# Row-wise logsumexp on one core: one Ln of ScalarE moved from before the last exp to after it, with the load sizes and shares redrawn

## The chip, the core and the metric

The kernel runs on one core of a Trainium2 chip. The metric is the device time of one execution in microseconds (us); of a kernel, the median of its runs. Three parts of the core do the work here: the 16 DMA engines bring the input from HBM into SBUF (the on-chip memory of 128 partitions), ScalarE (ACT in the profile) takes exponentials and logarithms, and VectorE (DVE) adds up rows. SyncE (SP) issues the transfers. TensorE has no part in it, and GpSimd (POOL) only sets a few constants at the start.

## What is computed

The input is `x`, 32 x 512 rows of 1024 fp32 numbers, and the output is one number for each row:

```python
x_max = np.max(x, axis=axis, keepdims=True)
return x_max.squeeze(axis) + np.log(np.sum(np.exp(x - x_max), axis=axis))
```

The kernel computes `log(sum(exp(x)))` without taking the maximum off; for the numbers drawn (standard normal) this is the same value. There are 16384 rows, 67.1 MB, and each partition holds 128 rows that lie one after the other in HBM. So a "row" below means one row in each of the 128 partitions: 4 KB per partition, 0.5 MB in all.

## The kernel before

The 128 rows are cut into 17 loads ("chunks") by the list `CHUNKS` (lines 11 to 16). An entry `(r, n_dve, parts, by_halves)` says: the chunk has `r` rows; VectorE sums the first `n_dve` of them, after ScalarE has exponentiated them in `parts` pieces; ScalarE sums the other `r - n_dve` itself, one row at a time. Early chunks have up to 16 rows, the last four have one row each.

*The ring.* The chunks land in `ring`, 51 rows of SBUF (line 54). The loop on lines 76 to 81 places them one behind the other and begins again at row 0 when a chunk doesn't fit. `load(i)` (lines 92 to 102) is issued on SyncE's queue. It first waits until whatever sat in its rows has been summed: for `dve_done` (VectorE's count of finished sums) or `act_done` (ScalarE's count of finished instructions), as the list `busy` noted. All loads share this one queue and are issued in order. Each has a semaphore of its own, `landed[i]`.

*The work on a chunk* (lines 126 to 172) is issued in program order on each engine; there is no scheduler, the order is written out by hand. ScalarE waits for `landed[i]` (line 135) and runs `exp` in place on the rows of each piece (line 137). VectorE waits for that piece and sums it, with one `reduce_sum` over all its rows (line 157), or, if `by_halves` is set, with one instruction per row (line 144) that adds the two halves of the row and accumulates the result; in the profile the latter is a CUSTOM_DVE_ANT_0 with a short DVE_READ_ACCUMULATOR2_ANT behind it. For the rows that ScalarE keeps, `exp` has an accumulator output (line 164): an ACTIVATE of 1024 elements and an ACTIVATION_READ_ACCUMULATOR that writes the row's sum. These sums go to `sums` in SBUF, except for the last `LATE` = 4 rows, whose sums go to `late` in PSUM (lines 111 to 115), a second on-chip memory.

*The logarithms.* `take_logs` (lines 104 to 109) puts on ScalarE's queue a wait for `act_done`, a wait for `dve_done` and a `Ln` of a stretch of sums, written to `res`. There are three:

- ahead of chunk `LN_AT` = 7, for the rows of chunks 0 to 5 (81 rows; lines 130 to 132);
- ahead of the last chunk, for all rows since then but the last four (43 rows; lines 133 and 134). Its `act_done` wait is for what was done before the first of the last four chunks, its `dve_done` wait for all of VectorE's sums;
- after the last chunk, for the last four rows (line 174). It waits for the last sum.

Then SyncE waits for the full count of `act_done` and stores `res`, 64 KB, with one transfer (lines 175 and 176). The activation tables for Exp and Ln are loaded once (line 122), and the load of chunk 0 is moved ahead of the start barrier (lines 184 to 192).

Of the kernel before, what the change touches and what calls it, by code (L numbers as in the profile page):

```python
# [8 lines left out]


CHUNKS = [
    (4, 4, 1, False), (15, 15, 1, False), (16, 16, 2, False), (16, 16, 2, False),
    (16, 15, 2, False), (14, 14, 2, False), (13, 12, 2, False), (9, 8, 1, False),
    (7, 7, 1, True), (5, 4, 1, True), (4, 3, 1, True), (3, 3, 1, False), (2, 2, 1, True),
    (1, 0, 1, False), (1, 0, 1, False), (1, 0, 1, False), (1, 0, 1, False),
]
RING_ROWS = 51

LN_AT = 7
LN_LAG = 1  # L20


LATE = 4


@with_exitstack
def kernel(
    ctx: ExitStack,
    tc: tile.TileContext,
    x: bass.AP,  # L30
    axis: bass.AP,
    out: bass.AP,
):
    nc = tc.nc
    P = nc.NUM_PARTITIONS

    assert axis in (-1, len(x.shape) - 1), f"only last-axis reduction supported, got {axis}"

    x_flat = x.flatten_outer_dims()
    N, D = x_flat.shape  # L40
    assert N % P == 0
    NB = N // P
    assert sum(r for r, *_ in CHUNKS) == NB

    fp32 = mybir.dt.float32
    Exp = mybir.ActivationFunctionType.Exp
    Ln = mybir.ActivationFunctionType.Ln
    Add = mybir.AluOpType.add
    AX = mybir.AxisListType.X

    x_v = x_flat.rearrange("(p t) d -> p t d", p=P)
    out_v = bass.AP(tensor=out.tensor, offset=out.offset, ap=[[NB, P], [1, NB]])

    ring = nc.alloc_sbuf_tensor("ring", [P, RING_ROWS, D], fp32).ap()
    sums = nc.alloc_sbuf_tensor("sums", [P, NB], fp32).ap()
    late = nc.alloc_psum_tensor("late", [P, 512], fp32).ap()
    res = nc.alloc_sbuf_tensor("res", [P, NB], fp32).ap()

    landed = [nc.alloc_semaphore(f"landed{i}") for i in range(len(CHUNKS))]
    act_done = nc.alloc_semaphore("act_done")  # L60
    dve_done = nc.alloc_semaphore("dve_done")
    stored = nc.alloc_semaphore("stored")
    used = sorted(sem.num for sem in [*landed, act_done, dve_done])
    assert used == list(range(used[0], used[0] + len(used)))

    tc.close()
    tc.compile()  # L70
    symbolic, nc._always_lower_symbolic_ap = nc._always_lower_symbolic_ap, False


    place = []
    row = slot = 0
    for r, *_ in CHUNKS:
        if slot + r > RING_ROWS:
            slot = 0
        place.append((slot, row))
        slot += r  # L80
        row += r

    busy = [(0, 0)] * RING_ROWS
    acts = dves = 0

    def cuts(n, parts):
        ends = [-(-n * k // parts) for k in range(parts + 1)]
        return [(lo, hi) for lo, hi in zip(ends, ends[1:]) if lo < hi]  # L90

    def load(i):
        (s, row), r = place[i], CHUNKS[i][0]
        act_wait = max(a for a, _ in busy[s : s + r])
        dve_wait = max(d for _, d in busy[s : s + r])
        if dve_wait:
            nc.sync.wait_ge(dve_done, dve_wait)
        if act_wait:
            nc.sync.wait_ge(act_done, act_wait)
        nc.sync.dma_start(out=ring[:, s : s + r], in_=x_v[:, row : row + r]).then_inc(  # L100
            landed[i], 16
        )

    def take_logs(lo, hi, src, dve_wait, act_wait):
        nonlocal acts
        nc.scalar.wait_ge(act_done, act_wait)
        nc.scalar.wait_ge(dve_done, dve_wait)
        nc.scalar.activation(out=res[:, lo:hi], in_=src, func=Ln).then_inc(act_done, 1)  # L108
        acts += 1

    late_row = place[-LATE][1]
    assert not any(n_dve for _, n_dve, _, _ in CHUNKS[-LATE:])

    def total(t):
        return late[:, t - late_row : t - late_row + 1] if t >= late_row else sums[:, t : t + 1]

    body = nc.main_func.blocks[-1]
    n_barrier = len(body.instructions)
    load(0)
    n_early = len(body.instructions)  # L120

    nc.scalar.preload_act_table_set("natural_log_exp_and_others")  # L122

    logged = 0
    done_before = [(0, 0)]
    for i, (r, n_dve, parts, by_halves) in enumerate(CHUNKS):
        if i:
            load(i)
        s, row = place[i]
        if i == LN_AT:  # L130
            logged = place[i - LN_LAG][1]
            take_logs(0, logged, sums[:, :logged], *done_before[i - LN_LAG])
        if i == len(CHUNKS) - 1:
            take_logs(logged, late_row, sums[:, logged:late_row], *done_before[-LATE])
        nc.scalar.wait_ge(landed[i], 16)
        for lo, hi in cuts(n_dve, parts):
            nc.scalar.activation(  # L137
                out=ring[:, s + lo : s + hi], in_=ring[:, s + lo : s + hi], func=Exp
            ).then_inc(act_done, 1)
            acts += 1  # L140
            nc.vector.wait_ge(act_done, acts)
            if by_halves:
                for j in range(lo, hi):
                    nc.vector.tensor_tensor_reduce(  # L144
                        out=ring[:, s + j, : D // 2],
                        in0=ring[:, s + j, : D // 2],
                        in1=ring[:, s + j, D // 2 :],
                        scale=1.0,
                        scalar=0.0,
                        op0=Add,  # L150
                        op1=Add,
                        accum_out=sums[:, row + j : row + j + 1],
                    ).then_inc(dve_done, 1)
                    dves += 1
                    busy[s + j] = (0, dves)
            else:
                nc.vector.reduce_sum(  # L157
                    out=sums[:, row + lo : row + hi], in_=ring[:, s + lo : s + hi], axis=AX
                ).then_inc(dve_done, 1)
                dves += 1  # L160
                for j in range(lo, hi):
                    busy[s + j] = (0, dves)
        for j in range(n_dve, r):
            nc.scalar.activation(  # L164
                out=ring[:, s + j],
                in_=ring[:, s + j],
                func=Exp,
                accum_out=total(row + j),
            ).then_inc(act_done, 1)
            acts += 1  # L170
            busy[s + j] = (acts, 0)
        done_before.append((dves, acts))

    take_logs(late_row, NB, late[:, : NB - late_row], dves, acts)
    nc.sync.wait_ge(act_done, acts)
    nc.sync.dma_start(out=out_v, in_=res).then_inc(stored, 16)


    nc.sync.sem_clear(range(used[0], used[-1] + 1))
    nc.sync.wait_ge(stored, 16)  # L180
    nc.sync.sem_inc(stored, -16)


    first = nc.main_func.blocks[0]
    head, work = first.instructions, body.instructions
    for ins in work[n_barrier:n_early]:
        at = next(
            k for k, i in enumerate(head) if i.engine == ins.engine and i.opcode == "Drain"
        )
        head.insert(at, ins)  # L190
    first.instructions = head
    body.instructions = work[:n_barrier] + work[n_early:]

    nc._always_lower_symbolic_ap = symbolic
# [33 lines left out]
```

The softmax here doesn't subtract the row's maximum and nothing guards it: scores larger than these inputs give would overflow.

## Time and profile before

| what | value |
|---|---|
| median of 9 runs | 162.32 us (162.24 to 162.68) |
| the profiled execution's own time | 162.32 us |
| its span, first to last instruction | 161.0 us |
| VectorE busy | 121.0 us, 46 instructions |
| ScalarE busy | 115.1 us, 40 instructions |
| packets of the load and store queue, share of 16 DMA engines' span | 97.2% |
| input read, mean rate over the span | 67.11 MB, 417 GB/s |
| chain that ended last | DMA 48%, DVE 29%, ACT 20% |

How to read it: the span is what the profile sees, and 1.3 us of the execution's own time lie around it. An engine's busy time is the time in which it had at least one instruction running. The chain of waits is followed back from the last instruction, at each step to what released it; its shares say which engine was the late one at that step, and a transfer that had been issued long before still counts from its issue. In the timeline each line is a start and a duration in us, and the text in brackets says how long the engine had been idle before it and what ended the idle time. Instructions on one engine overlap a little at their ends, so the distance from one start to the next is somewhat shorter than a duration.

### The profile page before, as it was taken

How to read it: one execution, taken by the hardware profiler on the slowest of the kernel's cores; microseconds unless marked ns; L12 is line 12 of the kernel's file. 1: busy time of each engine (PE TensorE's matmuls, PEld its weight loads, DVE VectorE, ACT ScalarE, POOL GpSimd, SP SyncE). 2: the span in 40 equal slices, each digit the busy share in tenths (PEclk: the TensorE clock that was granted, in tenths of full speed). 3: DMA queues.
4: the chain of work that ended last, by engine and by line, in shares of the span. 5: the costliest groups of instructions: out<-in, count | busy, mean ns of one | idle time of the engine just before them, and what ended most of it. 6: DMA issues, size and time to landing. Idle time of an engine off the chain costs nothing.

```text
span 161.0 us, 149 instructions
## 1 busy us (share of the span) xinstructions
DVE 121.0 (75%) x46; ACT 115.1 (71%) x40; POOL 0.2 (0%) x4
## 2 busy tenths in 40 slices
DVE  0028000003999999999999699999999999999892
ACT  3170006995089960999429993999199999999995
POOL 0000000000000000000000000000000000000000
DMA  7999889979979979979979999999999999999990
GB/s 273 493 488 473 366 382 521 456 326 521 456 326 521 440 342 521 440 342 521 440 309 456 456 456 440 423 423 423 422 421 421 433 442 401 436 415 428 407 402 29
DMA packets 2592, 67.18 MB, mean 417 GB/s; under 512 B 288, under 2 KB 416, under 8 KB 928
## 3 DMA queue, kind: packets, MB, share of 16 engines
q1 hardware_dynamic: 2592, 67.18, 97.2%
HBM read 67.11 MB, written 0.07 MB: 417 GB/s over the span
## 4 chain that ended last, share of the span: by engine, by line
DMA 48%; DVE 29%; ACT 20%; issue 0%
DMA ring<-in_x_dram 48%; DVE sums L157 29%; ACT ring L137 17%; ACT ring L164 3%; ACT res L108 0%
## 5 line engine op out<-in xcount | busy, mean ns | idle before, releaser
L157 DVE TENSOR_REDUCE sums<-ring 128x8 f32<-128x8192 f32 (+5 forms) x14 | 111.2, 7994 | 36.9 <-ACT ring L137 36.8
L137 ACT ACTIVATE ring<-ring 128x8192 f32<-128x8192 f32 (+6 forms) x18 | 104.4, 5835 | 42.9 <-DMA ring<-in_x_dram 42.8
L144 DVE CUSTOM_DVE_ANT_0 ring<-ring 128x512 f32<-128x512 f32 x16 | 9.9, 684 | 0.0
L164 ACT ACTIVATE ring<-ring 128x1024 f32<-128x1024 f32 x9 | 9.3, 1041 | 0.0
L122 ACT ACT_TABLE_LOAD x1 | 1.3, 1283 | 1.4 <-PEq L70 1.4
L164 ACT ACTIVATION_READ_ACCUMULATOR ring<-ring 128x1 f32 x9 | 1.6, 173 | 0.0
L144 DVE DVE_READ_ACCUMULATOR2_ANT sums<- 128x1 f32 x16 | 1.3, 80 | 0.0
L108 ACT ACTIVATE res<-sums 128x81 f32<-128x81 f32 (+1 forms) x2 | 0.5, 247 | 0.0
L108 ACT ACTIVATE res<-late 128x4 f32<-128x4 f32 x1 | 0.2, 174 | 0.0
L209 POOL MEMSET const-bfloat16-1.0<- 128x1 bf16 x1 | 0.1, 102 | 0.0
L209 POOL MEMSET const-uint8-127<- 128x1 uint8 x1 | 0.1, 102 | 0.0
L209 POOL MEMSET const-float32-0.0<- 128x1 f32 x1 | 0.1, 99 | 0.2 <-issue 0.2
L209 POOL MEMSET const-float32-1.0<- 128x1 f32 x1 | 0.1, 99 | 0.0
## 6 DMA issues: line engine op xcount, KB each, us to landing
ring<-in_x_dram SPq DMA_DIRECT2D x1, 7680.0 KB, 24.2
ring<-in_x_dram SPq DMA_DIRECT2D x1, 7168.0 KB, 28.6
ring<-in_x_dram SPq DMA_DIRECT2D x1, 6656.0 KB, 35.7
ring<-in_x_dram SPq DMA_DIRECT2D x1, 4608.0 KB, 20.3
ring<-in_x_dram SPq DMA_DIRECT2D x2, 2048.0 KB, 16.1
ring<-in_x_dram SPq DMA_DIRECT2D x1, 3584.0 KB, 28.3
ring<-in_x_dram SPq DMA_DIRECT2D x1, 2560.0 KB, 27.3
ring<-in_x_dram SPq DMA_DIRECT2D x4, 512.0 KB, 27.1
```

Source lines behind the costliest of these rows:

```text
L108: nc.scalar.activation(out=res[:, lo:hi], in_=src, func=Ln).then_inc(act_done, 1)
L122: nc.scalar.preload_act_table_set("natural_log_exp_and_others")
L137: nc.scalar.activation(out=ring[:, s + lo : s + hi], in_=ring[:, s + lo : s + hi], func=Exp).then_inc(act_done, 1)
L144: nc.vector.tensor_tensor_reduce(out=ring[:, s + j, : D // 2], in0=ring[:, s + j, : D // 2], in1=ring[:, s + j, D // 2 :], scale=1.0, scal ...
L157: nc.vector.reduce_sum(out=sums[:, row + lo : row + hi], in_=ring[:, s + lo : s + hi], axis=AX).then_inc(dve_done, 1)
L164: nc.scalar.activation(out=ring[:, s + j], in_=ring[:, s + j], func=Exp, accum_out=total(row + j),).then_inc(act_done, 1)
L209: nc = _bacc.Bacc("TRN2", target_bir_lowering=False, num_devices=1)
```

## The change

Two things are changed. The `Ln` that stood ahead of the last chunk now stands after the last chunk's `exp`, directly ahead of the last `Ln`; `LATE` goes from 4 to 3, so it covers 45 rows and the last one three. And `CHUNKS` has other sizes, pieces and shares.

```diff
 CHUNKS = [
-    (4, 4, 1, False), (15, 15, 1, False), (16, 16, 2, False), (16, 16, 2, False),
-    (16, 15, 2, False), (14, 14, 2, False), (13, 12, 2, False), (9, 8, 1, False),
-    (7, 7, 1, True), (5, 4, 1, True), (4, 3, 1, True), (3, 3, 1, False), (2, 2, 1, True),
-    (1, 0, 1, False), (1, 0, 1, False), (1, 0, 1, False), (1, 0, 1, False),
+    (4, 4, 1, False), (16, 16, 1, False), (16, 16, 1, False), (13, 13, 1, False),
+    (16, 14, 2, False), (15, 14, 2, False), (10, 10, 2, False), (11, 8, 1, False),
+    (7, 6, 1, False), (6, 6, 1, True), (4, 4, 1, True), (3, 3, 1, True), (2, 2, 1, True),
+    (2, 2, 1, True), (1, 0, 1, False), (1, 0, 1, False), (1, 0, 1, False),
 ]
-LATE = 4
+LATE = 3
...
         if i == LN_AT:
             logged = place[i - LN_LAG][1]
             take_logs(0, logged, sums[:, :logged], *done_before[i - LN_LAG])
-        if i == len(CHUNKS) - 1:
-            take_logs(logged, late_row, sums[:, logged:late_row], *done_before[-LATE])
         nc.scalar.wait_ge(landed[i], 16)
...
         done_before.append((dves, acts))
 
-    take_logs(late_row, NB, late[:, : NB - late_row], dves, acts)
+    last_sum = acts
+
+    take_logs(logged, late_row, sums[:, logged:late_row], *done_before[-1 - LATE])
+    take_logs(late_row, NB, late[:, : NB - late_row], dves, last_sum)
     nc.sync.wait_ge(act_done, acts)
```

There are still 17 loads. The rows that ScalarE sums itself go from nine to ten: seven into `sums` (two of chunk 4, one of chunk 5, three of chunk 7, one of chunk 8) and three into `late`. The moved `Ln` waits for the same things as before: all of VectorE's sums, and ScalarE's own before the last `LATE` chunks.

## The prediction

> **What bounds the kernel now.** I read the DMA part of the page first, then the chain of waits, then the timeline of the last microseconds. The page:
>
> ```profile
> DMA  7999889979979979979979999999999999999990
> q1 hardware_dynamic: 2592, 67.18, 97.2%
> HBM read 67.11 MB, written 0.07 MB: 417 GB/s over the span
> ```
>
> The DMA engines are busy from the first slice to the 39th. The input arrives without a break, and no engine's work is on the path unless it delays a load or follows the last one. The waits of ScalarE say the same (42.8 us on loads). The gaps between the starts of exps that a landing released give the pace: 83.68 - 64.32 = 19.36 us for a load of 16 rows, 116.35 - 100.62 = 15.73 for 13.
>
> The end of the chain, and what the trace says of the load that is issued last:
>
> ```profile
> 122.03 24.72 DMA ring<-in_x_dram
> 146.75 0.02 issue
> 146.78 2.76 ACT ring L137
> 149.54 1.04 ACT ring L164 x2
> 150.58 4.45 ACT ring L137 x2
> 155.03 3.01 ACT ring L164 x6
> 158.05 0.03 ACT res L108
> ...
> 158.08 1.11 ACT ring L164 x2
> 159.19 0.02 issue
> 159.21 0.17 ACT res L108
> ```
>
> ```profile
> L100 SPq DMA_DIRECT2D ring<-in_x_dram x1: 475/475/475, 129.8 to 129.8; - x1
> DMA to landing us min/median/max: 28.2/28.2/28.2
> ```
>
> The chain runs through ScalarE from 146.75 on and through the Ln of line 108 ahead of the last exp, as if that Ln were in the way. But the last load lands at 129.8 + 28.2 = 158.0 (158.03 in the trace's record of semaphores, from which all landings below are). An exp released by a landing starts 0.03 later, so the last one could start at 158.06, and it starts at 158.08. ScalarE and the last load meet: the Ln costs 0.02 us.
>
> ```profile
> 157.76 0.08 DVE L144 DVE_READ_ACCUMULATOR2_ANT sums<- 128x1 f32 x1
> 157.88 0.17 ACT L164 ACTIVATION_READ_ACCUMULATOR ring<-ring 128x1 f32 x1
> 157.93 0.24 ACT L108 ACTIVATE res<-sums 128x43 f32<-128x43 f32 x1
> 158.08 1.04 ACT L164 ACTIVATE ring<-ring 128x1024 f32<-128x1024 f32 x1
> 159.03 0.15 ACT L164 ACTIVATION_READ_ACCUMULATOR ring<-ring 128x1 f32 x1
> 159.21 0.17 ACT L108 ACTIVATE res<-late 128x4 f32<-128x4 f32 x1
> 159.41 0.35 SPq L176 DMA_DIRECT2D out_dram<-res  x1
> ```
>
> Here the reader is to see starts: Ln to next exp 0.15 us, exp to its accumulator read 0.95, read to the moved-to-be Ln 0.05, read to the last Ln 0.18 (the wait for the sum), Ln to store 0.20, store to the end of the span 1.59. From the last exp's start to the end are 2.92 us.
>
> **What the Trainium skill says.** "ScalarE: Activation LUTs", What ACT_TABLE_LOAD costs: an ACTIVATE with immediate scale and bias takes 186 ns and 0.833 ns per element, and neighbours overlap by 93 ns. The trace agrees: 8192 elements took 7022 ns, and 7010 come out. So from start to start an exp of r rows is an estimated 0.853 r + 0.093 us by that page (trace: 6.92 for 8, 6.06 for 7, 1.80 for 2). The same page, Step-by-step, has ScalarE faster to PSUM than to SBUF: the accumulator reads took 0.15 to 0.17 into PSUM and 0.18 to 0.19 into SBUF. "DMA: Bandwidth & Descriptors", Latency and other measured facts, gives about 0.6 us to the first byte of a transfer from SyncE; here the first packet came 1.0 us after the first issue, so I use the trace.
>
> **The loads.** The last four one-row loads took (158.03 - 152.96)/4 = 1.27 us each; with 19.36 for 16 rows this is 1.206 us a row and 0.06 a load. There are 17 loads and 128 rows in both kernels, so the last landing stays at 158.03. Taking the sizes that differ one by one (14, 9, 5, 1 go; 11, 10, 6, 2 come) gives at most +0.05. This holds if no load is issued late. A load goes out when its ring rows are summed. VectorE's sums, by start to start: 8.59 us for 8 rows, 7.52 for 7, 6.46 for 6, so 1.066 r + 0.06, with 0.09 more to the end.
> - Chunk 4 needs chunk 1's sum. Landing of 20 rows 7.47 + 19.36 = 26.83; exp of 16 rows 13.84 (the page's estimate; 15 rows took 13.00) to 40.7; sum of 16 rows 17.2 to 58.0. The load before it (49 rows against 51 by 64.30) lands at 61.9. Lead 3.9 us; in the kernel before it was 64.30 - 54.84 = 9.5.
> - Chunk 5 needs chunk 2's sum: landing 46.2, exp to 60.05, sum to 77.3. Queue empty at 83.65 - 2 x 1.206 = 81.2. Lead 3.9.
> - Chunk 6 goes out at 91.2 against 99.4, chunk 7 at 106.3 against 111.5, later ones 11 us or more ahead.
>
> What a lead must cover is the lag from an issue to the full flow. The first load shows it: 4 rows landed at 7.47, less 4.9 of data, 2.6 us. So 3.9 is enough, by 1.3. Cost nothing; without that cover, each microsecond of lag costs one.
>
> **ScalarE's work.** From the landing of chunk 7 (101 rows; 103 were in at 127.25, so 124.84) it has no idle time left. Exp start 124.87; then from start to start: 8 rows 6.92, three single sums at 1.04 (126.80 to 127.84) 3.12, 6 rows 5.22, one sum 1.04, 6 rows 5.22, 4 rows 3.51, 3 rows 2.65, twice 2 rows 3.60, two late sums at 1.00 (154.94 to 155.94) 2.00. Sum 33.28, so the last exp starts at 158.15. The landings on the way, worked out like chunk 7's, are always earlier (chunk 13: 154.23 against ScalarE at 154.35). The last landing would allow 158.06 to 158.11. So ScalarE is again level with the last load: +0.07 against 158.08. The tail of ScalarE is not shorter: it gave up one Ln (0.15) and took on as much exp.
>
> **The moved Ln.** The step moves one wait for VectorE and one ACTIVATE past one exp and one accumulator read on ScalarE's queue. It issues no DMA and passes nothing on the queues of SP or POOL. Removed ahead of the last exp: 0.15, already in the sum above. Added behind it: the wait for VectorE has only the last Ln and the store queued behind it. VectorE, busy without a break from 60.1, ends its last sum at an estimated 157.6 (16, 13, four of 7, two of 5, 8 and 6 rows as above: 147.0; fifteen halved rows at 0.613 to 156.3; the last two, released by ScalarE at about 156.2, to 157.6). The Ln could start at 158.15 + 0.95 + 0.05 = 159.15, so 1.5 us cover the wait. The Ln of three rows must wait for the last sum anyway: read from 159.10 to 159.25, released at about 159.28. The moved Ln starts at 159.15 and lets it go 0.15 later, 159.30. So it lies in the gap that the last sum leaves (0.18 from read to Ln before); it adds between 0 and 0.15, and I take 0.02. LATE from 4 to 3 changes nothing in this: a Ln of 4 took 174 ns.
>
> **The sum.** Last Ln at 159.30 against 159.21: +0.09, of which 0.07 is ScalarE's later last exp and 0.02 the moved Ln. The profiled execution took 162.32 us, its span 161.00 and 1.32 around it; this is exactly the median of the 9 runs (162.24 to 162.68). 162.32 + 0.09 = 162.41. About 0.2% (0.32 us) is what a measurement of this kernel can tell from no change; this lies inside.
>
> **The rivals.**
> - *The move pays.* If ScalarE's shares make it 0.1 us earlier than I sum, the last exp is bound by the landing alone (158.06), and the moved Ln fits wholly: 162.30. The sums of durations leave room for this, but nothing more can be had while the last load lands at 158.03. Chance 8%.
> - *ScalarE's sums don't overlap.* Chunk 7 has three single sums in a row into SBUF. The kernel before never has two there one after the other; its pairs write to PSUM. If one has to let the read before it finish, the step costs 1.04 + 0.19 = 1.23, twice: +0.38, and as there is no idle time behind, all of it reaches the end: 162.79. Against it: the exp and the Ln behind such a read started 0.10 after the read's start, in the middle of it. Bounds for the pair: 1.00 (as in PSUM) to 1.23; I take 1.04. Chance 9%.
> - *The load queue runs dry* (the one on the other side). Place: chunks 4 and 5, whose sums are now one instruction of 16 rows. It decides when the lag from issue to full flow is over 3.9 us; then the end moves by the excess, once, since a late chunk 4 gives chunk 5 the same time back. At a lag of 5 us: 163.5. For it: no load in the kernel before is issued with so little ahead of it, the first excepted. Against it: that first one needed 2.6. Chance 5%.
> - *The new sizes stream faster.* Loads of 10 and 11 rows are not in the trace before; to end under 162.0 they would have to save 0.4 us, against a straight line through all sizes shown. Chance 2%.
> - *The change doesn't do what it says.* Excluded as far as the order goes: in the built program both Ln stand behind the last exp. "Shorter tail" is what I find not to be true.
>
> **How the numbers follow.** Likeliest, 76%: 162.41, its own range 162.25 to 162.6 (0.15 for the Ln's upper bound, the rest for durations summed over 33 us and the spread of a median). Faster 3%: the streaming case and a remnant. Slower by over 0.2%, 14%: the sums that don't overlap and the dry queue. Within, 83%. The range 162.22 to 162.75 leaves out the dry queue, the streaming case and about half of the non-overlapping sums.
>
> **What would show it.** Right: the DMA row without a gap, last landing at 158.0 to 158.1, no idle time of ScalarE after the landing of chunk 7 at 124.8, last exp at 158.1 to 158.2, moved Ln right behind the accumulator read, last Ln 0.2 us after that read's start, and loads 4 and 5 issued at 58.0 and 77.3. Wrong: a DMA gap near 62 or 81 us; steps of 1.2 us within chunk 7's sums; a wait for VectorE ahead of the moved Ln; or a last landing that has moved by more than 0.1.

## The result and the profile after

The changed kernel took 163.17 us (median of 9 runs, 162.88 to 163.37), the kernel before 162.31 (median of 29, 162.19 to 162.88). The ratio is 1.0046, 95% interval 1.0037 to 1.0055: slower by 0.86 us. The prediction was 162.41, its range ended at 162.75. The profiled execution of the changed kernel took 162.91 us, with a span of 161.58; that is at the lower end of its runs.

The DMA part of its page, to be set against the three lines of before:

```profile
DMA  7997997997999999799899998999899999999990
q1 hardware_dynamic: 2592, 67.18, 97.0%
HBM read 67.11 MB, written 0.07 MB: 416 GB/s over the span
```

There is no hole to be seen: the share of busy time fell from 97.2 to 97.0%. The end of the timeline:

```profile
157.67 1.04 ACT L161 ACTIVATE ring<-ring 128x1024 f32<-128x1024 f32 x1
158.03 0.08 DVE L141 DVE_READ_ACCUMULATOR2_ANT sums<- 128x1 f32 x1
158.62 0.15 ACT L161 ACTIVATION_READ_ACCUMULATOR ring<-ring 128x1 f32 x1
158.67 1.04 ACT L161 ACTIVATE ring<-ring 128x1024 f32<-128x1024 f32 x1
159.62 0.15 ACT L161 ACTIVATION_READ_ACCUMULATOR ring<-ring 128x1 f32 x1
159.67 0.23 ACT L107 ACTIVATE res<-sums 128x45 f32<-128x45 f32 x1
159.80 0.17 ACT L107 ACTIVATE res<-late 128x3 f32<-128x3 f32 x1
160.00 0.35 SPq L176 DMA_DIRECT2D out_dram<-res  x1
```

The last exp starts at 158.67 instead of 158.08. From there on both kernels are alike: 1.13 us to the last Ln, 0.20 to the store. The moved Ln lies inside the gap between the accumulator read and the last Ln, which is 0.18 us long with or without it. So the 0.58 us by which the span grew were lost before the last exp. The chain says where to look:

```profile
60.06 46.21 DVE sums L154 x4
106.27 0.02 issue
106.29 19.09 DMA ring<-in_x_dram
125.38 0.02 issue
125.40 7.03 ACT ring L134
132.43 3.12 ACT ring L161 x6
...
159.77 0.20 ACT res L107 x2
```

From the landing of chunk 7 the chain is ScalarE without a pause, and that landing is at 125.38, not at 124.84 as forecast. The delay of 0.54 was there already at chunk 4. The view of the transfers gives the issue of load 4 and its time to landing, first for the changed kernel, then for the one before:

```profile
L99 SPq DMA_DIRECT2D ring<-in_x_dram x1: 328/328/328, 58.0 to 58.0; - x1
DMA to landing us min/median/max: 23.8/23.8/23.8
```

```profile
L100 SPq DMA_DIRECT2D ring<-in_x_dram x1: 328/328/328, 54.8 to 54.8; - x1
DMA to landing us min/median/max: 28.8/28.8/28.8
```

Before: chunk 3 landed at 64.30, chunk 4 at 83.65, 19.35 us later, the time of 16 rows. After: chunk 3 at 61.89, chunk 4 at 81.78, 19.89 later. The packets of the trace show how: each of the 16 DMA engines moves 8 packets of a 16-row load, 2.42 us each when they follow one another. The first packets of load 4 took 2.44 to 2.71 us, and the engines began them on the mean 0.17 us after their last packet of load 3 (0.002 in the kernel before). The next load, issued at 77.3, lost no more. This is the rival of the dry queue, at its place, but at a lead at which the prediction saw 1.3 us to spare.

### The profile page after: what moved, and what is told of

Same layout as the page of the kernel before. It is cut to its first block, busy times and chain, and to the rows that moved or that the text cites. A ratio compares the mean times of both kernels' runs of the same rounds, so it can differ in the third digit from the quotient of the medians.

```text
span 161.6 us, 151 instructions
## 1 busy us (share of the span) xinstructions
DVE 119.3 (74%) x46; ACT 115.0 (71%) x41; POOL 0.2 (0%) x4
## 4 chain that ended last, share of the span: by engine, by line
DMA 39%; ACT 30%; DVE 29%; SPq 0%; issue 0%
DMA ring<-in_x_dram 39%; DVE sums L154 29%; ACT ring L134 25%; ACT ring L161 4%; SPq L99 0%; ACT res L107 0%
## 5 line engine op out<-in xcount | busy, mean ns | idle before, releaser
L154 DVE TENSOR_REDUCE sums<-ring 128x7 f32<-128x7168 f32 (+6 forms) x12 | 108.8, 9124 | 38.8 <-ACT ring L134 38.8
L134 ACT ACTIVATE ring<-ring 128x7168 f32<-128x7168 f32 (+8 forms) x17 | 103.3, 6116 | 43.6 <-DMA ring<-in_x_dram 43.6
L141 DVE CUSTOM_DVE_ANT_0 ring<-ring 128x512 f32<-128x512 f32 x17 | 10.6, 684 | 0.0
L161 ACT ACTIVATE ring<-ring 128x1024 f32<-128x1024 f32 x10 | 10.3, 1040 | 0.0
L107 ACT ACTIVATE res<-sums 128x80 f32<-128x80 f32 (+1 forms) x2 | 0.5, 244 | 0.0
```

Of the source, the lines that this page charges most:

```text
L134: nc.scalar.activation(out=ring[:, s + lo : s + hi], in_=ring[:, s + lo : s + hi], func=Exp).then_inc(act_done, 1)
L141: nc.vector.tensor_tensor_reduce(out=ring[:, s + j, : D // 2], in0=ring[:, s + j, : D // 2], in1=ring[:, s + j, D // 2 :], scale=1.0, scal ...
L154: nc.vector.reduce_sum(out=sums[:, row + lo : row + hi], in_=ring[:, s + lo : s + hi], axis=AX).then_inc(dve_done, 1)
L161: nc.scalar.activation(out=ring[:, s + j], in_=ring[:, s + j], func=Exp, accum_out=total(row + j),).then_inc(act_done, 1)
```

## The experiments

In what follows the lead of a load is the time from its issue to the landing of the load ahead of it, and its loss is how much later than 19.35 us (16 rows) or 18.14 (15 rows) after that landing it lands; both are of the profiled execution. Lead and loss together are the time from issue to landing less the time of the data. That is the measure by which the prediction read a lag of 2.6 us off the first load; where nothing is lost, it is only an upper bound. The span is given as the median of all runs of a kernel, because the time around it is not the same for all (last section). The kernel before has a span of 161.0, the changed one 161.8. The theory is that a load issued only 3.9 us ahead costs the time; the rivals are ScalarE's tail, the place of the Ln, and the sizes as such.

**The two halves of the change.** First its front alone, in the kernel before:

```diff
-    (4, 4, 1, False), (15, 15, 1, False), (16, 16, 2, False), (16, 16, 2, False),
-    (16, 15, 2, False), (14, 14, 2, False), (13, 12, 2, False), (9, 8, 1, False),
+    (4, 4, 1, False), (16, 16, 1, False), (16, 16, 1, False), (13, 13, 1, False),
+    (16, 14, 2, False), (16, 14, 2, False), (13, 12, 2, False), (9, 8, 1, False),
```

> The kernel before with only the front of the change: chunks 1 to 3 are 16, 16 and 13 rows in one piece each; chunks 4 to 6 are 16, 16, 13 with 14, 14, 12 rows for VectorE; from chunk 7 on, the Ln and LATE as in the kernel before. Theory, late loads: leads of 3.9 us for loads 4 and 5 as in the changed kernel, so slower than the kernel before by about as much as the changed one: 162.8 to 163.2, with last landing near 158.5. Rivals (Ln, ScalarE's tail): 162.3, as before.

Measured: 163.06 us, ratio 1.0050 (1.0036 to 1.0064), as slow as the whole change. Load 4 went out at 57.89 and landed 1.06 late; load 5, with a lead of 5.0, lost 0.01:

```profile
L100 SPq DMA_DIRECT2D ring<-in_x_dram x1: 328/328/328, 57.9 to 57.9; - x1
DMA to landing us min/median/max: 24.3/24.3/24.3
```

Then the tail alone, in the changed kernel:

```diff
-    (4, 4, 1, False), (16, 16, 1, False), (16, 16, 1, False), (13, 13, 1, False),
-    (16, 14, 2, False), (15, 14, 2, False), (10, 10, 2, False), (11, 8, 1, False),
+    (4, 4, 1, False), (15, 15, 1, False), (16, 16, 2, False), (16, 16, 2, False),
+    (16, 14, 2, False), (13, 12, 2, False), (10, 10, 1, False), (11, 8, 1, False),
```

> The changed kernel's other part alone: chunks 7 to 16, LATE and the place of the Ln as changed, but chunks 1 to 3 as in the kernel before (15, 16, 16 rows, two of them in two pieces), then 16, 13 and 10 rows. Loads 4 and 5 then go out 9.5 and 11.6 us ahead. Theory, late loads are what cost: 162.41, as predicted, span 161.1, last exp at 158.15, and within 0.15 us of the kernel before. Rival, ScalarE's tail or the Ln costs beside the loads: 162.6 or more.

Measured: 162.44 us, ratio 1.0005 (0.9996 to 1.0014), span 161.1. The new tail, LATE and the moved Ln together cost nothing that can be measured, and the time is the predicted one to 0.03 us, which is closer than the scatter of its runs (162.30 to 162.80) and so in part luck. Its load 4 was early again and lost nothing (chunk 3 at 64.25, chunk 4 at 83.59). The profiled execution has a span of 161.5, at the upper end: there chunks 5, 6 and 7 landed 0.5 us late in all (against rows times the pace), though their loads had been issued long before. Such scatter is in every kernel here, the one before too (162.19 to 162.88).

**Repairing the loads.** Chunk 1 alone, then chunks 1 and 2 in two pieces, in the changed kernel:

```diff
-    (4, 4, 1, False), (16, 16, 1, False), (16, 16, 1, False), (13, 13, 1, False),
+    (4, 4, 1, False), (16, 16, 2, False), (16, 16, 1, False), (13, 13, 1, False),
```

> The changed kernel with chunk 1 worked in two pieces of 8 rows instead of one of 16; nothing else. Theory, late loads: load 4 then goes out at 51, 10.8 us ahead of the empty queue, and lands on time (81.2 instead of 81.8). But load 5 still waits for the one-piece sum of chunk 2 and goes out at 77.3, now with a lead of 3.9 us instead of 4.5, so the queue runs dry there instead: no gain, 162.9 to 163.3 us, with the dip of the DMA engines near 81 us and chunk 5 landing 0.5 late. Rival, only load 4 was late: 162.4. Rival, the end is set by ScalarE's shares or by the moved Ln and not by loads: as the changed kernel, 163.17, with the dip still at 61 us or none.

Measured: 162.54 us, ratio 1.0012 (1.0005 to 1.0019). This is outside the expected 162.9 to 163.3 and nearer to the rival's 162.4. Load 5 did become the late one, with a lead of 3.94, but it lost 0.27, about half of what load 4 had lost at the same lead. So most of the time came back with load 4 alone.

The same for chunk 2 as well, `(16, 16, 2, False)`:

> The changed kernel with chunks 1 and 2 both in two pieces. Theory, late loads: loads 4 and 5 go out about 11 and 7 us or more ahead, no DMA dip, last landing 158.0, and the time becomes what was predicted for the changed kernel with no dry queue, 162.41 (162.3 to 162.55). Rival, ScalarE's tail or the moved Ln made it slower: still 163.0 to 163.2. Rival, other load sizes stream worse: still over 162.8.

Measured: 162.78 us, ratio 1.0029 (1.0021 to 1.0038), above the forecast. In the profile all is as the theory has it: loads 4 and 5 at 51.0 and 70.4, last landing 157.84, span 160.9. The median span is 161.2, near the kernel before. But around the span lie 1.59 us in this kernel, against 1.3 in the kernel before and the changed one. So the kernel is no clean repair; the tail alone, with 1.31 around its span, is.

**The place of the Ln**, in the kernel with both chunks in two pieces:

```diff
+        if i == len(CHUNKS) - 1:
+            take_logs(logged, late_row, sums[:, logged:late_row], *done_before[-LATE])
         nc.scalar.wait_ge(landed[i], 16)
...
-    take_logs(logged, late_row, sums[:, logged:late_row], *done_before[-1 - LATE])
```

> Chunks 1 and 2 in two pieces, and the Ln of 45 rows back ahead of the last exp; the rest as the changed kernel. This prices the moved Ln alone where no load is late. Theory: ScalarE has no idle time in the tail, so a Ln ahead of the last exp delays it by 0.15: last exp at 158.3, 0.13 us more than with the Ln behind, 162.54. Rival, the last landing decides: the same time as with the Ln behind, within 0.05. Rival, the moved Ln is what costs: 0.2 us or more faster than with the Ln behind.

Measured: 162.79 us, ratio 1.0027 (1.0017 to 1.0038); the medians don't separate the two. The profiles do, by the tail after the last landing. With the Ln behind, that landing was at 157.84; with it ahead, at 158.07:

```profile
157.97 1.04 ACT L161 ACTIVATE ring<-ring 128x1024 f32<-128x1024 f32 x1
158.92 0.15 ACT L161 ACTIVATION_READ_ACCUMULATOR ring<-ring 128x1 f32 x1
158.97 0.23 ACT L107 ACTIVATE res<-sums 128x45 f32<-128x45 f32 x1
159.10 0.17 ACT L107 ACTIVATE res<-late 128x3 f32<-128x3 f32 x1
```

```profile
158.24 0.23 ACT L107 ACTIVATE res<-sums 128x45 f32<-128x45 f32 x1
158.37 1.04 ACT L163 ACTIVATE ring<-ring 128x1024 f32<-128x1024 f32 x1
159.31 0.15 ACT L163 ACTIVATION_READ_ACCUMULATOR ring<-ring 128x1 f32 x1
159.50 0.17 ACT L107 ACTIVATE res<-late 128x3 f32<-128x3 f32 x1
```

With the Ln ahead, the last exp starts 0.13 us after the Ln (158.37 against 158.24), where it could have started itself; everything behind the exp takes the same time in both. So in this tail, where ScalarE has no time to spare, the move is worth 0.13 us, by one profiled execution of each and as the expectation had it. From the landing to the last Ln are 1.26 us with the Ln behind and 1.43 with it ahead; 0.04 of this difference is where the landing fell. The redrawn shares spend the gain: the kernel before, with the Ln ahead, has 1.18.

**How much lead a load needs.** Both chunks in two pieces, chunk 2's exp row by row, and load 4 held back until the n-th of these is done (n from 11 to 15):

```diff
+        if i == 4:
+            act_wait = max(act_wait, 3 + 11)
...
+            for a in range(lo, hi) if i == 2 else [lo]:
+                b = a + 1 if i == 2 else hi
...
```

> Chunks 1 and 2 in two pieces (so that load 5 is early), chunk 2's exp row by row (16 instructions, for a finely graded count), and load 4 made to wait for the 11th of them. It should go out at about 56.7, 5.1 us before the load ahead of it has landed. Theory, a load needs some 4 us of lead: nothing lost, chunk 4 lands 19.35 us after chunk 3, span about 161.1. Rival, the one-piece sums of 16 rows cost by themselves and the lead doesn't matter down to 2.6 us: the same.

> As the kernel with the 11th, but load 4 waits for the 12th exp of chunk 2: issue at about 57.7, lead 4.1 us. Theory, a load needs some 4 us: on the edge, chunk 4 lands 0 to 0.4 us late, span 161.1 to 161.5. Rival, lead doesn't matter down to 2.6: nothing lost.

> Load 4 waits for the 13th exp of chunk 2: issue at about 58.6, lead 3.2 us. Theory, a load needs some 4 us: chunk 4 lands 0.8 to 1.2 us late and the span is 161.9 to 162.3. Rival, lead doesn't matter down to 2.6: nothing lost.

> Load 4 waits for the 14th exp of chunk 2: issue at about 59.5, lead 2.3 us. Theory, a load needs some 4 us: chunk 4 lands 1.6 to 2.1 us late, span 162.7 to 163.2; from one kernel of this row to the next the loss grows by the step of the issue, 0.95 us. Rival, lead doesn't matter down to 2.6: 0.3 us lost.

> Load 4 waits for the 15th exp of chunk 2: issue at about 60.4, lead 1.4 us, half a microsecond ahead of the first engine running out. Theory, the lag from issue to full flow is about 2.6 us when the engines fall idle (first load, and the load at a lead of 2.3 us) and 4 to 4.6 us while they are busy: here they are idle, full flow at 60.4 + 2.7 = 63.1 against 61.4, 1.7 us lost, span 162.6 to 162.9. Rival, a lag of 4 us in every case: flow at 64.5, 3 us lost, span 164.

Two more points came from doing the first ten rows in pairs, which brings the count earlier. The first of them was meant for 59.0 and went out at 58.2, so that it fills the row but doesn't test what it was made for:

> Load 4 goes out at about 59.0, between the kernels at 58.6 and at 59.5: lead 2.8 us. (Chunk 2's exp is ten rows in pairs and six single rows, so that the count comes then.) Theory, the lag shortens as the engines fall idle: a loss between 0.8 and 1.4 us, span 161.8 to 162.5, so the fall from 1.4 to 0.8 is one slope and not a chance of one kernel. Rival, the order of 1.4 at 58.6 and 0.8 at 59.5 is chance: anything, 1.5 or more included.

> The load that was meant for 59.0 and went out at 58.2, now one exp later: issue at about 59.15, lead 2.7 us, between the kernels at 58.6 (1.4 us lost) and 59.5 (0.8 lost). Theory, the lag shortens as the engines run out: 0.8 to 1.4 us lost, span 161.8 to 162.5. Rival, the low loss at 59.5 is chance and the loss grows with lateness throughout: 1.8 or more lost, span 162.8 or more.

| issue of load 4, us | lead | loss | lead + loss | span, profiled | span, median | ratio to before (interval) |
|---|---|---|---|---|---|---|
| 56.68 (n = 11) | 5.1 | 0.00 | at most 5.1 | 160.9 | 161.0 | 1.0017 (1.0007 to 1.0028) |
| 57.70 (12) | 4.3 | 0.15 | 4.5 | 161.6 | 161.5 | 1.0051 (1.0036 to 1.0066) |
| 57.95 (changed kernel) | 3.9 | 0.54 | 4.5 | 161.6 | 161.8 | 1.0046 (1.0037 to 1.0055) |
| 58.21 (pairs) | 3.7 | 0.33 | 4.0 | 161.4 | 162.15 | 1.0069 (1.0048 to 1.0090) |
| 58.59 (13) | 3.2 | 1.39 | 4.6 | 162.3 | 162.4 | 1.0110 (1.0093 to 1.0127) |
| 59.34 (pairs) | 2.7 | 0.81 | 3.5 | 162.0 | 162.1 | 1.0059 (1.0041 to 1.0076) |
| 59.52 (14) | 2.3 | 0.75 | 3.0 | 161.7 | 161.8 | 1.0072 (1.0057 to 1.0087) |
| 60.52 (15) | 1.3 | 1.53 | 2.8 | 162.6 | 162.7 | 1.0106 (1.0074 to 1.0137) |

Each ratio is to the kernel before as it ran beside that kernel. The kernels of this table, the changed one apart, have 1.6 us around their span, and the kernel before was itself at 161.3 to 161.4 in the runs beside the two with pairs and the one with n = 15; so median spans of these are to be read 0.3 lower. The profiled execution of the point at 58.21 was the fastest of its eight (span 161.4, median 162.15), so 0.33 is not its usual loss.

The load with n = 11 took 24.5 us from issue to landing; the one with n = 13, 23.9; the one with n = 14, issued a microsecond later than that, 22.4:

```profile
L101 SPq DMA_DIRECT2D ring<-in_x_dram x1: 327/327/327, 56.7 to 56.7; - x1
DMA to landing us min/median/max: 24.5/24.5/24.5
```

```profile
L101 SPq DMA_DIRECT2D ring<-in_x_dram x1: 328/328/328, 58.6 to 58.6; - x1
DMA to landing us min/median/max: 23.9/23.9/23.9
```

```profile
L101 SPq DMA_DIRECT2D ring<-in_x_dram x1: 328/328/328, 59.5 to 59.5; - x1
DMA to landing us min/median/max: 22.4/22.4/22.4
```

So it is shown that a late issue of load 4 alone costs the time: with n = 11 the kernel has the sizes of the changed one and the span of the kernel before, and with n = 13 it has 1.4 us more. A lead of 5.1 us loses nothing, and neither does load 5 of the changed kernel at 4.5; 3.2 lose 1.4. At 4.3 the 0.15 lost in the profile is no more than loads 3 and 5 lost there (0.14 and 0.20), which had been issued 44 and 10 us ahead; the median span is 0.5 longer all the same, and the profile doesn't tell what of that is load 4's.

It is not one lag. At leads of 3.2 to 3.9 a load needed 4.0 to 4.6 us by the column of sums (5.0 in the front alone, 4.2 for load 5 with chunk 1 in two pieces), at 2.7 and less 2.8 to 3.5, nearer to the 2.6 of the first load. The theory that the loss grows by the step of the issue failed at n = 14; that the fall from 1.4 to 0.8 is real was borne out by the point at 2.7, and that a need of 4 us doesn't hold on idle engines by n = 15. But the reason that the expectations give, engines that run out, fits n = 15 alone. There they stood idle for 0.7 to 1.1 us between the packets of load 3 and those of load 4. At 2.7 and 2.3 they went on to load 4 within 0.004 and 0.04 us on the mean, and its first packets took 2.42 to 3.24 and 2.46 to 3.06 us; with n = 13, after a mean of 0.05, 2.76 to 3.74. The landing is that of the slowest engine: up to the end of their first packets the 16 had lost 0.73 us on the mean with n = 13, and 0.19 at 2.7, where the loss of the whole load is 0.81.

**Packets.** A guess on why was that a load must be out before an engine begins its last packet of the load ahead, 1.97 us long for 13 rows and 2.42 for 16. Then a short last packet would help. The changed kernel with loads 3 and 4 as 11 + 2 and 14 + 2 rows, and n = 13 with load 3 as 11 + 2 (`parts_of_load` gives the pieces of a load):

```diff
-        nc.sync.dma_start(out=ring[:, s : s + r], in_=x_v[:, row : row + r]).then_inc(
-            landed[i], 16
-        )
+        for lo, hi in parts_of_load(i):
+            nc.sync.dma_start(
+                out=ring[:, s + lo : s + hi], in_=x_v[:, row + lo : row + hi]
+            ).then_inc(landed[i], 16)
...
-        nc.scalar.wait_ge(landed[i], 16)
+        nc.scalar.wait_ge(landed[i], 16 * len(parts_of_load(i)))
...
```

> The changed kernel with loads 3 and 4 each sent as two transfers, 11 + 2 and 14 + 2 rows, so that the last packet that each DMA engine moves before load 4 or 5 is one of 2 rows (0.31 us) and not of 13 or 16 (1.98, 2.42). Loads 4 and 5 go out as late as in the changed kernel (58.0 and 77.3). Theory, a load must be out about 1 us before an engine begins its last packet: lead is enough now, first packets of chunk 4 at full speed, chunk 4 lands on time, span 161.2 to 161.3 (two more transfers cost 0.06 each). Rival, a fixed lead of about 4 us is needed whatever runs ahead: still 0.5 to 1 us lost, span 161.6 to 162.

> The kernel whose load 4 waits for the 13th exp of chunk 2 (issue at 58.6, lead 3.2 us, span 162.4), with load 3 sent as 11 + 2 rows. Theory, a load must be out about 1 us before an engine begins its last packet: most of the 1.4 us come back, span 161.1 to 161.4. Rival, fixed lead of about 4 us: still 162.2 to 162.5.

> The same kernel (issue at 58.6) with load 4 itself sent as 2 + 14 rows and load 3 whole. If the loss belongs to the packet that runs ahead: the first packets of chunk 4 are slow again, span 162.2 to 162.6. If it belongs to the long first packet of the late load: gone, span 161.1 to 161.4.

Measured: 162.95 us, ratio 1.0031 (1.0020 to 1.0042), span 161.6 with a wide scatter of 161.1 to 162.3; 164.10, ratio 1.0094 (1.0071 to 1.0118), span 162.5; and with load 4 as 2 + 14 rows 163.95, ratio 1.0094 (1.0080 to 1.0107), span 162.35. In the first, load 4 lost 0.5 us, as in the changed kernel (a transfer more counted as 0.06). In the two with n = 13 the span is as long as without the split (162.4), and load 4 lost 1.45 and 1.2 us against 1.39, so neither the length of the packets ahead nor that of the first packet makes it. The guess has fallen. In the third, the short first packets themselves took up to 1.39 us instead of 0.31.

## Why the prediction was wrong

It failed in one step: "What a lead must cover is the lag from an issue to the full flow. The first load shows it: 4 rows landed at 7.47, less 4.9 of data, 2.6 us. So 3.9 is enough, by 1.3." The lag was taken from the first load, which starts on idle engines, and used for one that is issued while all 16 are moving data. By the same measure, issue to landing less the time of the data, the late loads at leads of 3.2 to 3.9 needed 4.0 to 5.0 us: 4.5 for load 4 of the changed kernel, so 3.9 was short by 0.54. The rival of the dry queue had the place right and also the rule that the loss comes once (load 5 lost nothing after load 4 had lost 0.54). It had the lag from which it decides wrong, and so was given 5%. Of the signs that the prediction named, a last landing moved by more than 0.1 came (158.55), and a gap in the DMA row did not, though load 4 was late.

The other terms, by the profiled execution:

- *Issues of the loads.* Forecast 58.0, 77.3, 91.2, 106.3; measured 57.95, 77.31, 91.24, 106.29.
- *ScalarE from chunk 7 to the last exp.* Forecast 33.28 us, measured 158.67 - 125.40 = 33.27.
- *Three single sums in a row.* They start at 132.34, 133.37 and 134.41: 1.04 each, so that rival (1.23) is out.
- *The moved Ln.* Forecast 0.02, bounds 0 and 0.15; measured 0.00, the last Ln 0.18 after the start of the accumulator read as before. VectorE was done at 158.11, 1.56 us ahead of it (forecast 1.5).
- *The tail as a whole.* From the last landing (158.55) to the last Ln 1.25 us against 1.18: +0.07, forecast +0.09. The tail alone gave 162.44 for a forecast of 162.41.
- *Landings.* Forecast 158.03 to 158.08, measured 158.55; all of the difference came at chunk 4.

The sum for the profiled execution is 0.52 (landing) + 0.07 (tail) = 0.59, with 0.59 measured (162.91 against 162.32 for the one before). The median lies 0.26 higher still. That the loss at load 4 differs from one execution to the next would explain it: at the same lead of 3.9 it was 0.27, 0.54 and 1.06 in three kernels. But the other executions have no trace, so this is argued and not shown.

Where the expected gain of a shorter tail went: there was 0.02 us to be had, since the last load lands when ScalarE is ready for it. No kernel tried here is faster than the one before; the tail alone is level with it.

What stays open is why such a load needs 4 to 5 us. That the engines are busy at its issue isn't shown to be the reason: they were just as busy at leads of 2.7 and 2.3, where it needed 3.5 and 3.0. The Trainium skill, "DMA: Bandwidth & Descriptors", Latency and other measured facts, says that HBM access takes 0.2 us on average and 2 us at high load. That fits the direction of 2.6 us for the first load against 4.0 to 5.0, but not the fall below a lead of 3.2, and no run here separates HBM from the making of the descriptors.

## What to carry to other kernels

Where DMA is the bound, list for each load its lead over the end of the load ahead, and look for the smallest one; a change of piece sizes that makes the sum which frees the ring rows longer can cut it, though it adds no busy time. Take the lag that the lead must cover from a load issued while the engines are busy, not from the first one: here 5.1 us of lead lost nothing and 3.9 lost 0.3 to 1.1. And don't look for the loss in the busy row: a good part of it is in packets that take longer, and it is seen as landings that come later than rows times the pace.

## What else the runs showed

- The DMA busy share hardly moves when a load is late: 97.0% with 0.54 us lost, 97.2% before. Of the time that the engines lost on load 4, 0.17 us on their mean lie between packets; the rest is inside packets, which count as busy. First packets of load 4 took up to 2.71 us here, and up to 3.74 with n = 13, instead of 2.42.
- The time around the span is not fixed: 1.31 to 1.36 us in the kernels of up to 153 instructions, 1.59 to 1.66 in those of 155 and more. Two kernels with the same median span of 161.2 took 162.54 and 162.78 us for this. What sets it was not tested.
- A load issued later can land earlier: with n = 14 load 4 was issued 0.93 us later than with n = 13 and landed at 81.89 instead of 82.53, behind a load 3 that had landed at the same time in both (61.78 and 61.79).
